# Softmax over rows of 1024: twelve rows per partition and four buffers, in place of eight rows and six

## The chip, the cores and the metric

The kernel runs on one core of a Trainium2 chip. The metric is the device time of one execution in microseconds (us). The kernel before takes 317.45 us, the median of three runs that lie between 317.37 and 318.42 us.

## What is computed

The input `x` has 32 x 512 rows of 1024 float32 numbers, 64 MiB in all, and the temperature is 0.5. Each row is divided by the temperature and goes through a softmax that subtracts the row's maximum first. The output has the shape and type of the input.

```python
scaled = x / temperature
shifted = scaled - np.max(scaled, axis=-1, keepdims=True)
exp_x = np.exp(shifted)
return exp_x / np.sum(exp_x, axis=-1, keepdims=True)
```

So 67.1 MB are read from HBM, 67.1 MB are written to it, and each element is touched by three computations: the maximum, the exponential with its sum, and the multiplication by the sum's reciprocal.

## The kernel before

**Tiles.** The 16384 rows are cut into 16 tiles of 1024 rows. A tile lies in SBUF as 128 partitions with 8 rows each, 32 KiB per partition. The 8 rows of a partition are neighbours in HBM too, so that each partition's share of a transfer is one contiguous piece of 32 KiB (`dram`, L49). Six buffers of this size (`BUFS`, L11) are used in turn, and everything is done in place: a tile is loaded, computed and stored from the same buffer.

**Passes.** A tile is computed in one pass of eight rows, or, for the first two and the last two tiles, in two passes of four (`PASSES`, L13). A pass consists of four steps:

- `maximum` (L62): DVE reduces the rows of the pass to one maximum per row (L68) and scales it to a bias (L71).
- `exponential` (L73): ACT takes one row per instruction (L77) and gives the row's sum as well.
- `divide` (L86): DVE takes the reciprocals (L89), and multiplies the rows by them. Tiles in `WHOLE` (L15: 2, 4, 6, 8, 10 and 12) are multiplied by one instruction for all rows of the pass (L92, TENSOR_TENSOR). Other tiles take one instruction for each row (L95, TENSOR_SCALAR).
- `store` (L99): after the last pass of a tile, ACT's queue issues the store of the whole tile (L107), and the next load is put in order. The very first pass has a store of its own: POOL's queue stores the first row of each partition of tile 0 (L104), so that the store of tile 0 has seven rows.

**Order.** The order is written out by hand. First SP issues six loads (L59). Then, for each pass in turn, the maximum and exponential of this pass come ahead of the division and store of the pass before. From tile 14 on (`ALONE`, L17), the division and the store of the tile before come first when a new tile begins. [...] A load stands on SP and waits until the store of the tile that had its buffer has landed.

**Queues.** Loads run in SP's DMA queue (q1 in the profile), stores in ACT's (q10), and the one piece in POOL's (q0).

Of the kernel before, what the change touches and what calls it, by code (L numbers as in the profile page):

```python
# [1 line left out]

# [4 lines left out]

ROWS = 8  # L10
BUFS = 6  # L11

PASSES = [[4, 4]] * 2 + [[8]] * 12 + [[4, 4]] * 2  # L13

WHOLE = (2, 4, 6, 8, 10, 12)  # L15

ALONE = 14  # L17


@with_exitstack  # L20
def kernel(
    ctx: ExitStack,
    tc: tile.TileContext,
    x: bass.AP,
    temperature: bass.AP,
    out: bass.AP,
):
    nc = tc.nc
    f32 = mybir.dt.float32
    scale = 1.0 / float(temperature)  # L30
    extreme = mybir.AluOpType.max if scale > 0 else mybir.AluOpType.min

    P = 128
    xf = x.flatten_outer_dims()
    of = out.flatten_outer_dims()
    n, d = xf.shape
    assert len(PASSES) * ROWS * P == n

    data = ctx.enter_context(tc.tile_pool(name="data", bufs=BUFS))
    stats = ctx.enter_context(tc.tile_pool(name="stats", bufs=4))  # L40


    groups = []
    for i, ks in enumerate(PASSES):
        assert sum(ks) == ROWS
        for j, k in enumerate(ks):
            groups.append((i, sum(ks[:j]), k))

    def dram(t, i):  # L49
        block = t[P * ROWS * i : P * ROWS * (i + 1), :]  # L50
        return block.rearrange("(p k) d -> p k d", p=P, k=ROWS)

    tiles, small = [], []

    def load():
        i = len(tiles)
        if i < len(PASSES):
            xt = data.tile([P, ROWS, d], f32, name="xt")
            nc.sync.dma_start(out=xt, in_=dram(xf, i))  # L59
            tiles.append(xt)  # L60

    def maximum(g):  # L62
        i, a, k = groups[g]
        top, bias, sums, recip = (
            stats.tile([P, k], f32, name=name) for name in ("top", "bias", "sums", "recip")
        )
        small.append((bias, sums, recip))
        nc.vector.tensor_reduce(  # L68
            out=top, in_=tiles[i][:, a : a + k, :], axis=mybir.AxisListType.X, op=extreme
        )  # L70
        nc.vector.tensor_scalar_mul(bias, in0=top, scalar1=-scale)  # L71

    def exponential(g):  # L73
        i, a, k = groups[g]
        bias, sums, _ = small[g]
        for b in range(k):
            nc.scalar.activation(  # L77
                tiles[i][:, a + b, :],
                tiles[i][:, a + b, :],
                mybir.ActivationFunctionType.Exp,  # L80
                bias=bias[:, b : b + 1],
                scale=scale,
                accum_out=sums[:, b : b + 1],
            )

    def divide(g):  # L86
        i, a, k = groups[g]
        _, sums, recip = small[g]
        nc.vector.reciprocal(recip, sums)  # L89
        if i in WHOLE:  # L90
            xt = tiles[i][:, a : a + k, :]
            nc.vector.tensor_mul(xt, xt, recip.unsqueeze(2).to_broadcast([P, k, d]))  # L92
            return
        for b in range(k):
            nc.vector.tensor_scalar_mul(  # L95
                tiles[i][:, a + b, :], in0=tiles[i][:, a + b, :], scalar1=recip[:, b : b + 1]
            )

    def store(g):  # L99
        i, a, k = groups[g]  # L100


        if g == 0:
            nc.gpsimd.dma_start(out=dram(of, i)[:, :1, :], in_=tiles[i][:, :1, :])  # L104
        elif a + k == ROWS:
            a = 1 if i == 0 else 0
            nc.scalar.dma_start(out=dram(of, i)[:, a:, :], in_=tiles[i][:, a:, :])  # L107
            load()

    with tc.manual_schedule():
        for _ in range(BUFS):
            load()
        for g in range(len(groups) + 1):

            alone = g < len(groups) and groups[g][0] >= ALONE and groups[g][1] == 0
            if g > 0 and alone:
                divide(g - 1)
                store(g - 1)  # L120
            if g < len(groups):
                maximum(g)
                exponential(g)
            if g > 0 and not alone:
                divide(g - 1)
                store(g - 1)


# [1 line left out]
_INS = ['x', 'temperature']  # L130
_OUTS = [((32, 512, 1024), 'float32')]

_NUMBERS = {'temperature': 0.5}


# [26 lines left out]
```

## Time and profile before

| | before |
|---|---|
| median of 3 runs | 317.45 us |
| the profiled execution | 317.44 us |
| its span, from the first to the last instruction or transfer | 315.7 us |
| DVE busy | 251.0 us, 79% |
| ACT busy | 148.1 us, 47% |
| moved over the span | 134.24 MB, mean 425 GB/s |

The profile is of one execution. Its costliest groups of instructions are below. Each line gives the source line, the engine, the operation, what it writes and reads (partitions x elements), how many there are, the busy time in us, the mean of one in ns, and behind the second bar how long the engine had been idle before them and what ended most of that.

```profile
L77 ACT ACTIVATE xt<-xt,bias 128x1024 f32<-128x1024 f32 x128 | 145.2, 1135 | 136.6 <-DVE bias L71 127.1 <-issue 9.6
L68 DVE TENSOR_REDUCE top<-xt 128x8 f32<-128x8192 f32 x12 | 104.2, 8684 | 31.2 <-DMA xt<-in_x_dram 31.2
L95 DVE TENSOR_SCALAR xt<-xt,recip 128x1024 f32<-128x1024 f32 x80 | 54.3, 748 | 0.5
L92 DVE TENSOR_TENSOR xt<-xt,recip 128x8192 f32<-128x8192 f32 x6 | 52.2, 8692 | 0.2
L68 DVE TENSOR_REDUCE top<-xt 128x4 f32<-128x4096 f32 x8 | 35.3, 4412 | 13.2 <-DMA xt<-in_x_dram 13.2
```

A row multiplied by its own TENSOR_SCALAR starts some 0.67 us after the one before (5.39 us for eight), since they overlap a little. In the single TENSOR_TENSOR a row takes 1.09 us.

### The profile page before, as it was taken

The numbers are of one execution on the slowest core, as the hardware profiler recorded it, in microseconds if no ns is written. First come the engines' busy times: TensorE is split into PE (matmuls) and PEld (weight loads), VectorE is DVE, ScalarE is ACT, GpSimd is POOL, SyncE is SP. The second block draws the span as 40 slices with busy tenths as digits, with TensorE's granted clock in tenths as the row PEclk, the third lists the DMA queues.
The fourth block names the chain that finished last, engine by engine and source line by source line (L and its number), as shares of the span: only waits on it lengthen the run. The fifth ranks groups of instructions, "written<-read, shape, count | busy, mean of one in ns | idle before, by whom it ended". The sixth has DMA issues, their size and how long they took to land. (4 is left out here: it accounts for less than half of the span.)

```text
span 315.7 us, 534 instructions
## 1 busy us (share of the span) xinstructions
DVE 251.0 (79%) x146; ACT 148.1 (47%) x257; POOL 1.3 (0%) x5
## 2 busy tenths in 40 slices
DVE  0399999999679795897949979399793999979710
ACT  0176637680906519074290833808247091564700
POOL 0001000000000000000000000000000000000000
DMA  8999999999999999999999999999999999999996
GB/s 328 415 448 421 369 441 434 465 400 461 404 457 407 457 411 457 428 436 436 428 448 415 448 415 449 411 465 403 461 403 461 403 461 403 461 403 461 407 457 274
DMA packets 4755, 134.24 MB, mean 425 GB/s; under 512 B 528, under 2 KB 528, under 8 KB 656
## 3 DMA queue, kind: packets, MB, share of 16 engines
q1 hardware_dynamic: 2304, 67.11, 49.7%
q10 hardware_dynamic: 2304, 66.59, 48.9%
q0 software_dynamic: 144, 0.52, 0.4%
q14 instruction: 3, 0.02, 0.0%
HBM read 67.11 MB, written 67.11 MB: 425 GB/s over the span
## 5 line engine op out<-in xcount | busy, mean ns | idle before, releaser
L77 ACT ACTIVATE xt<-xt,bias 128x1024 f32<-128x1024 f32 x128 | 145.2, 1135 | 136.6 <-DVE bias L71 127.1
L68 DVE TENSOR_REDUCE top<-xt 128x8 f32<-128x8192 f32 (+1 forms) x20 | 139.5, 6976 | 44.4 <-DMA xt<-in_x_dram 44.4
L95 DVE TENSOR_SCALAR xt<-xt,recip 128x1024 f32<-128x1024 f32 x80 | 54.3, 748 | 0.5
L92 DVE TENSOR_TENSOR xt<-xt,recip 128x8192 f32<-128x8192 f32 x6 | 52.2, 8692 | 0.2
L77 ACT ACTIVATION_READ_ACCUMULATOR xt<-xt,bias 128x1 f32 x128 | 23.9, 187 | 0.0
L77 ACT ACT_TABLE_LOAD x1 | 1.3, 1283 | 13.3 <-DMA xt<-in_x_dram 13.3
L89 DVE RECIPROCAL recip<-sums 128x8 f32<-128x8 f32 (+1 forms) x20 | 3.8, 188 | 4.1 <-ACT xt L77 4.1
L71 DVE TENSOR_SCALAR bias<-top 128x8 f32<-128x8 f32 (+1 forms) x20 | 3.4, 171 | 0.7
L104 POOL DMA_DIRECT2D out_dram<-xt x1 | 1.1, 1142 | 23.4 <-DVE xt L95 23.4
L143 POOL MEMSET const-bfloat16-1.0<- 128x1 bf16 x1 | 0.1, 96 | 0.0
L143 POOL MEMSET const-float32-0.0<- 128x1 f32 x1 | 0.1, 93 | 0.2 <-issue 0.2
L143 POOL MEMSET const-float32-1.0<- 128x1 f32 x1 | 0.1, 93 | 0.0
L143 POOL MEMSET const-uint8-127<- 128x1 uint8 x1 | 0.1, 93 | 0.0
## 6 DMA issues: line engine op xcount, KB each, us to landing
xt<-in_x_dram SPq DMA_DIRECT2D x16, 4096.0 KB, 51.2
out_dram<-xt ACTq DMA_DIRECT2D x15, 4096.0 KB, 28.0
out_dram<-xt ACTq DMA_DIRECT2D x1, 3584.0 KB, 23.2
out_dram<-xt POOLq DMA_DIRECT2D x1, 512.0 KB, 19.6
```

What stands on the lines that cost most here:

```text
L68: nc.vector.tensor_reduce(out=top, in_=tiles[i][:, a : a + k, :], axis=mybir.AxisListType.X, op=extreme)
L71: nc.vector.tensor_scalar_mul(bias, in0=top, scalar1=-scale)
L77: nc.scalar.activation(tiles[i][:, a + b, :], tiles[i][:, a + b, :], mybir.ActivationFunctionType.Exp, bias=bias[:, b : b + 1], scale=scal ...
L89: nc.vector.reciprocal(recip, sums)
L92: nc.vector.tensor_mul(xt, xt, recip.unsqueeze(2).to_broadcast([P, k, d]))
L95: nc.vector.tensor_scalar_mul(tiles[i][:, a + b, :], in0=tiles[i][:, a + b, :], scalar1=recip[:, b : b + 1])
L104: nc.gpsimd.dma_start(out=dram(of, i)[:, :1, :], in_=tiles[i][:, :1, :])
L143: nc = _bacc.Bacc("TRN2", target_bir_lowering=False, num_devices=1)
```

## The change

The tiles become larger and their number smaller: ten tiles of twelve rows per partition (pieces of 48 KiB), and a last one of eight rows. There are four buffers instead of six; four times twelve rows take as much of SBUF as six times eight. The first tile is computed in three passes of four rows, the next nine in two passes of six, the last in two passes of four. `WHOLE` names tiles 2, 3, 4, 6 and 8, whose multiplications are now one instruction per pass of six rows. `ALONE` is 9, so that the division and store of the tile before come first for the last two tiles.

Two things are new. Ahead of the store of tile 0, ACT copies one element per partition of tile 2 into a small tile (`seen`), and so waits for the load of tile 2. The stores of tiles 4 and 6 (`HALVES`) are issued as two DMAs each, one of partitions 0 to 63 and one of partitions 64 to 127.

```diff
-ROWS = 8
-BUFS = 6
+PASSES = [[4, 4, 4]] + [[6, 6]] * 9 + [[4, 4]]
+BUFS = 4
-PASSES = [[4, 4]] * 2 + [[8]] * 12 + [[4, 4]] * 2
+WHOLE = (2, 3, 4, 6, 8)
-WHOLE = (2, 4, 6, 8, 10, 12)
+ALONE = 9
-ALONE = 14
+HALVES = (4, 6)
...
+    rows = [sum(ks) for ks in PASSES]
...
     def dram(t, i):
-        block = t[P * ROWS * i : P * ROWS * (i + 1), :]
-        return block.rearrange("(p k) d -> p k d", p=P, k=ROWS)
+        block = t[P * sum(rows[:i]) : P * sum(rows[: i + 1]), :]
+        return block.rearrange("(p k) d -> p k d", p=P, k=rows[i])
...
-        elif a + k == ROWS:
+        elif a + k == rows[i]:
             a = 1 if i == 0 else 0
-            nc.scalar.dma_start(out=dram(of, i)[:, a:, :], in_=tiles[i][:, a:, :])
+            if i == 0:
+                nc.scalar.copy(stats.tile([P, 1], f32, name="seen"), tiles[2][:, 0, 0:1])
+            for p, q in ((0, 64), (64, P)) if i in HALVES else ((0, P),):
+                nc.scalar.dma_start(out=dram(of, i)[p:q, a:, :], in_=tiles[i][p:q, a:, :])
             load()
```

More of the change, by code (lines that the diff above doesn't have):

```diff
@@ L36 @@
     n, d = xf.shape
-    assert len(PASSES) * ROWS * P == n
+    rows = [sum(ks) for ks in PASSES]
+    assert sum(rows) * P == n
     data = ctx.enter_context(tc.tile_pool(name="data", bufs=BUFS))
@@ L44 @@
     for i, ks in enumerate(PASSES):
-        assert sum(ks) == ROWS
         for j, k in enumerate(ks):
@@ L57, in load @@
         if i < len(PASSES):
-            xt = data.tile([P, ROWS, d], f32, name="xt")
+            xt = data.tile([P, rows[i], d], f32, name="xt")
             nc.sync.dma_start(out=xt, in_=dram(xf, i))
```

## The prediction

> **What bounds the kernel now.** I read the head of the page first (span, engines, slices), then the DMA queues, then the same trace cut into stretches, then the waits.
>
> ```profile
> span 315.7 us, 534 instructions
> DVE 251.0 (79%) x146; ACT 148.1 (47%) x257; POOL 1.3 (0%) x5
> DMA  8999999999999999999999999999999999999996
> ...
> q1 hardware_dynamic: 2304, 67.11, 49.7%
> q10 hardware_dynamic: 2304, 66.59, 48.9%
> q0 software_dynamic: 144, 0.52, 0.4%
> ```
>
> No compute engine is full, but the DMA row is at 9 from the second slice to the last but one. The three queues (loads, stores, and the one piece that POOL stores) together took 99.0% of what 16 engines have in the span. The chain of waits covers only 18% of the span, since it ends at ACT and DVE work of the last tiles; here it is not the view that names the bound. The stretches show the rate:
>
> ```profile
> 0.00:2.00 2.00, 0.00 (x0) 0.00 (x0) 0.20 (x4) 1.00 0.67 180
> 2.00:37.00 35.00, 23.43 (x17) 15.09 (x25) 1.14 (x1) 1.00 1.00 417
> 37.00:280.00 243.00, 209.79 (x111) 122.59 (x215) 0.00 (x0) 1.00 1.00 432
> 280.00:312.00 32.00, 17.74 (x19) 10.40 (x19) 0.00 (x0) 1.00 0.99 428
> ```
>
> The columns are the stretch, its length, busy time of DVE, ACT and POOL, the clock, the DMA share and GB/s. Loads alone (second row), both directions (third) and stores alone (fourth) all run at a DMA share of 0.99 to 1.00 and close to one rate. A byte costs the same in either direction, and 134.2 MB at 432 GB/s is 310.7 us. What remains of the span is the 1.8 us before the first packet, 0.7 us by which the first packets are long, the piece of POOL, some 1.0 us by which the last DMA engine ends after the mean one (packet records: 314.5 against 313.5), and 1.2 us after the last packet.
>
> ```profile
> DVE top L68 <- DMA xt<-in_x_dram: 44.4, 10, 13.2
> ...
> SPq L59 <- DMA out_dram<-xt: 214.3, 10, 42.9
> ```
>
> ```profile
> 298.20 2.74 DVE L95 TENSOR_SCALAR xt<-xt,recip 128x1024 f32<-128x1024 f32 x4
> 300.97 0.34 ACTq L107 DMA_DIRECT2D out_dram<-xt  x1
> ```
>
> The first two lines are from the waits (total, times, longest), the last two from the timeline (start, length). DVE waits for loads (44.4 us) and the loads' queue waits for stores to free a buffer (214.3 us): everybody waits for the DMA engines. The last store is issued at 300.97, while the store before it still runs to 304.7 (packet records), so even at the end the engines are not kept waiting.
>
> [...] where both queues have work, the middle stretch, they take nearly equal shares. [...]
>
> **The change, part by part.**
>
> *Pieces of 48 KiB.* Packets: the loads' 2304 are 16 x 144, that is 128 pieces and 16 small ones per load. The packet records give 1213 ns for 32 KiB and 1062 ns for the 28 KiB pieces of the first store; the 4 KiB between them cost 151 ns, so 32 KiB need 1208 and about 5 ns are fixed per packet. One DMA engine moves 256 pieces now and 171 after: 85 x 5 ns = 0.4 us gained. A 48 KiB piece should take 1213 + 4 x 151 = 1817 ns. This is extrapolated; if pieces were cut in two, the 0.4 us is gone, nothing more.
>
> *DVE and ACT.* Rows and passes change, not the work per row. Multiplications in one instruction go from 48 rows to 60: 12 x (8.69/8 - 5.39/8) = 5.0 us more on DVE, which then has about 256 us in 316. In the steady part a tile of 12 rows has 12 x 2 pieces per partition, 8 partitions per engine: 16 x 1.817 = 29.1 us. DVE needs 2 x 6.55 (maxima, between 4.41 for 4 rows and 8.68 for 8) + 0.7 + 13.0 = 26.8 us for a tile multiplied whole and 21.9 for another, ACT 12 x 1.134 = 13.6. Both stay under 29.1, so the DMA engines remain the bound and the cost is 0.
>
> *Four buffers instead of six.* Both hold 48 rows. A steady buffer is loading for 29.1 us, storing for 29.1, computing for about 27; four times 29.1 leaves some 30 us over. A load that comes late doesn't idle the engines while the stores' queue has work.
>
> *The start.* This is the only place where both queues can run dry, and I follow it by shifting the first tiles' times. Load 0 ends 4.8 us later (8 x 0.604), so DVE starts at 18.05 instead of 13.21. With the durations of the timeline: maxima of passes 0 and 1 and the division of pass 0 to 30.3, maximum of pass 2 to 34.7, division of pass 1 to 37.7, first maximum of tile 1 to 44.2, division of pass 2 to 47.3. ACT does the six exponentials of that pass of tile 1 from 44.4 to 51.3. Only then come, in its queue, the new copy and the store of tile 0. The copy waits for load 2, which lands at 1.8 + 0.7 + 3 x 14.54 + 1.2 (POOL's piece) = 47.3; it is no wait at all and costs one small ACT instruction, about 0.2 us by the 187 ns row of 128x1. Were it to bind, the exponentials of tiles 1 and 2 would queue behind it, and DVE behind those. Store 0 goes out at 51.8 instead of 32.9. Until then only loads run, which costs nothing at equal rates. The four loads, POOL's piece and store 0 (11 rows, 8 x 1.666 = 13.3) together keep the engines busy to 1.8 + 0.7 + 58.2 + 1.2 + 13.3 = 75.2, in whichever order. Load 4 can't start before store 0 has landed, so store 1 must be there by 75.2. Its chain: maximum to 53.7, exponentials to 60.8, division of pass 0 to 58.2, maximum of tile 2 to 64.7, exponentials of tile 2 (ahead of the store in ACT's queue) to 71.7, store issued by 72.1. From issue to first packet the trace has 2.2 us (last store) to 3.8 (first store, behind packets in flight): 74.3 to 75.9. So it is 0.9 us early to 0.7 us late; I take 0, and 0.7 for the range.
>
> *Stores after that.* Store 1 ends at about 103, and store 2 is issued at 96; each later margin by the same sums is 9 us or more.
>
> *The end.* Load 10 follows store 6 and ends about 271. Then 3 us of store 7, stores 8 and 9 (14.5 each) and store 10 (9.7) are left, 42 us alone. The compute between the last landing and the last issue took 20 us before (281 to 301). Cost 0; the longer packets make the ends of the DMA engines more ragged, 0.2 us taken, 0 to 0.6 possible.
>
> *Two stores cut by partitions (tiles 4 and 6).* One more issue each, 0.34 us on ACT, hidden. [...] Worst: they move in step and each store packet takes twice as long: 8 packets x 2 tiles x 1.817 = 29 us. The records of before have often 13 engines in one phase and 3 in the other, which speaks for the worst[...]. I take 0 for the likeliest, because a figure for half the partitions alone says little of stores that have only half of each engine's time, and give the loss a case of its own.
>
> Sum on the profiled execution: 315.7 - 0.4 + 0 + 0.2 = 315.5. The run took 1.7 us more than its span (317.44 against 315.7) and equals the median 317.45, so 317.2.
>
> **Rivals.** *Half-partition stores collide* (slower): between 7 and 29 us as above; the middle[...] is 14.5 us, giving 331.7. It decides against "no change" once a split store's packet takes over 1817 + 1600/16 = 1.92 us. Against it: each engine has load packets in between.
> *The start runs dry, or long pieces run below 432 GB/s*: if store 1 is 2.5 us late at 75 us the time is 319.7; pieces 1% slower cost 3.1 us, 320.3. Against it: the sums above, and that 28 and 32 KiB pieces go at one rate.
> [...]
>
> **How the numbers follow.** Forecast 0.62 (its own range 316.2 to 318.5), collision 0.20, start or rate 0.14 (of it 0.03 within half a per cent)[...]. Half a per cent, about what a measurement can tell from no change, is 1.6 us: faster below 315.9, slower above 319.0. So faster 0.04, same 0.65, slower 0.31. [...]
>
> **What would show it.** DMA share 0.99 or more in every stretch from 3 to 310 us, above all around 75, and 432 GB/s in the middle: the forecast. A fall of GB/s between about 160 and 250 us, while tiles 4 and 6 are stored, with long packets there: the collision. A gap in the DMA share near 75: the start. Wrong altogether would be a time under 315, for which the engines would have to move bytes faster than any stretch of before does.

## The result and the profile after

The changed kernel takes 337.23 us (median of six runs), the kernel before 317.36 us beside it. That is 19.9 us slower, where 317.2 was forecast. Without the longest execution the loss is 19.4 us, a ratio of 1.061 with a 95% interval of 1.059 to 1.064. Executions of the changed kernel scatter, from 331.3 to 342.7 us over all that were made; the profile that came with the result is of the longest one (342.69 us), so a second one of the same kernel, 331.3 us long and made apart from the others, is read beside it.

First the head of the page of the first profile, then its DMA queues and the chain of waits by engine.

```profile
span 340.9 us, 517 instructions
...
DVE 257.1 (75%) x147; ACT 148.4 (44%) x258; POOL 1.3 (0%) x5
...
DMA  9999999999999999999999999999999999988780
GB/s 358 398 444 458 406 455 371 424 448 398 450 444 421 427 456 421 416 461 433 346 352 375 341 404 415 444 427 300 358 358 369 381 419 425 434 373 386 342 381 35
...
q10 hardware_dynamic: 1616, 66.59, 48.0%
q1 hardware_dynamic: 1584, 67.11, 47.4%
...
DMA 56%; DVE 27%; ACT 11%; issue 0%; DVEq 0%; SPq 0%
```

DVE's work is 257 us, close to the 256 of the prediction, and ACT's is 148 as before. The DMA row still shows 9 nearly to the end. But the row of GB/s has two dents, slices 20 to 23 and 28 to 32, about where the prediction looked for the sign of a collision (160 to 250 us; slices are 8.5 us long): the engines count as busy there and move 300 to 380 GB/s in place of some 430. From 160 to 200 us the share is 0.99 at 363 GB/s, from 100 to 160 it is 1.00 at 433: the share alone does not show the loss, and the two rows must be read together. The chain of waits leads through DMAs for 56% of the span, but that is no sign of the collision: in the changed kernel without the cut, the first experiment below, it is 51%.

The second profile in stretches (length, busy time of DVE, ACT and POOL, clock, DMA share, GB/s):

```profile
60.00:100.00 40.00, 39.79 (x18) 21.91 (x39) 0.00 (x0) 1.00 1.01 435
100.00:160.00 60.00, 56.04 (x20) 27.70 (x49) 0.00 (x0) 1.00 1.00 434
160.00:200.00 40.00, 28.22 (x19) 20.59 (x36) 0.00 (x0) 1.00 0.98 361
200.00:220.00 20.00, 15.45 (x5) 6.90 (x12) 0.00 (x0) 1.00 1.00 430
220.00:260.00 40.00, 33.62 (x24) 20.70 (x36) 0.00 (x0) 1.00 0.99 372
```

A piece is what a DMA moves for one partition, 48 KiB here, and has one packet in the profiler's records. By these records the two DMAs of tile 4 run from 161 to 201 us, and those of tile 6 are issued at 218 and have landed by 266. Of the stretches shown the rate is low in these two alone; from 60 to 100 us, where the start could have run dry, it is 435. A piece of 48 KiB takes 1.815 us elsewhere; in these two stretches the longest pieces of stores take 3.7 and 4.1 us, and those of the loads beside them lengthen too, to as much as 4.0. In the first profile seven pieces of tile 6 take 4.1 to 7.5 us, more than twice 1.815; why they do is open.

### The profile page after: what moved, and what is told of

It is laid out like the page before. It is cut to its first block, busy times and chain, and to the rows that moved or that the text cites. A ratio compares the mean times of both kernels' runs of the same rounds, so it can differ in the third digit from the quotient of the medians.

```text
span 340.9 us, 517 instructions
## 1 busy us (share of the span) xinstructions
DVE 257.1 (75%) x147; ACT 148.4 (44%) x258; POOL 1.3 (0%) x5
## 4 chain that ended last, share of the span: by engine, by line
DMA 56%; DVE 27%; ACT 11%; issue 0%; DVEq 0%; SPq 0%
DMA xt<-in_x_dram 30%; DMA out_dram<-xt 25%; DVE top L69 17%; ACT xt L78 11%; DVE xt L96 7%; DVE xt L93 2%; DVE bias L72 1%; DVE recip L90 0%; DVEq L163 0%; SPq L60 0%
## 5 line engine op out<-in xcount | busy, mean ns | idle before, releaser
L69 DVE TENSOR_REDUCE top<-xt 128x6 f32<-128x6144 f32 (+1 forms) x23 | 139.9, 6084 | 56.8 <-DMA xt<-in_x_dram 56.8
L93 DVE TENSOR_TENSOR xt<-xt,recip 128x6144 f32<-128x6144 f32 x10 | 65.6, 6558 | 0.6 <-DVE recip L90 0.3
L96 DVE TENSOR_SCALAR xt<-xt,recip 128x1024 f32<-128x1024 f32 x68 | 46.2, 749 | 0.5
L90 DVE RECIPROCAL recip<-sums 128x6 f32<-128x6 f32 (+1 forms) x23 | 4.2, 182 | 5.0 <-ACT xt L78 5.0
L72 DVE TENSOR_SCALAR bias<-top 128x6 f32<-128x6 f32 (+1 forms) x23 | 3.9, 171 | 0.8
## 6 DMA issues: line engine op xcount, KB each, us to landing
out_dram<-xt ACTq DMA_DIRECT2D x1, 4096.0 KB, 19.4
```

Source lines behind the costliest of these rows:

```text
L69: nc.vector.tensor_reduce(out=top, in_=tiles[i][:, a : a + k, :], axis=mybir.AxisListType.X, op=extreme)
L96: nc.vector.tensor_scalar_mul(tiles[i][:, a + b, :], in0=tiles[i][:, a + b, :], scalar1=recip[:, b : b + 1])
```

## The experiments

Two readings stood against each other. **C**: stores of 64 partitions that all lie on one side of partition 64 collide: their packets slow one another down. **S**: the start, the longer pieces or the four buffers cost the time. A third, **N**, is that two DMAs in place of one cost something, whatever they span.

### The changed kernel without the cut

```diff
-HALVES = (4, 6)
+HALVES = ()
```

> The changed kernel with HALVES empty: all stores span 128 partitions. Theory C [...]: the whole loss goes, 316.5 to 318. Rival S (the start, the longer pieces or four buffers cost the time): 325 or more remains. Both in part: between.

Measured: 318.07 us, 1.0024 times the kernel before (1.0012 to 1.0035). Of the 19.9 us, 19.2 go with the cut; S is left with 0.7. The profile of this kernel in the stretches in which tiles 4 and 6 were slow:

```profile
160.00:200.00 40.00, 30.71 (x23) 20.70 (x36) 0.00 (x0) 1.00 1.00 434
200.00:220.00 20.00, 19.86 (x10) 8.42 (x15) 0.00 (x0) 1.00 1.00 433
220.00:260.00 40.00, 34.85 (x20) 19.18 (x34) 0.00 (x0) 1.00 1.00 431
```

Both dents are gone, and the DMA share, 1.00, is hardly higher than with them.

### One cut store

```diff
-HALVES = (4, 6)
+HALVES = (4,)
```

> The changed kernel with the store of tile 4 alone cut by partitions. C, if each cut store costs the same: half of the 19.9 us, 326 to 329. If the second cut store meets DMA engines that the first has put out of step, the first costs less than half (under 325) or more (over 330). S: 337 as with both.

Measured: 326.47 us, 8.4 more than without a cut; the second cut adds 10.8. Its profile has one dent, where tile 4 is stored:

```profile
160.00:200.00 40.00, 28.15 (x19) 20.53 (x36) 0.00 (x0) 1.00 0.99 359
200.00:220.00 20.00, 15.55 (x5) 6.90 (x12) 0.00 (x0) 1.00 1.00 435
220.00:260.00 40.00, 34.43 (x24) 20.70 (x36) 0.00 (x0) 1.00 0.99 426
```

The dent accounts for the loss. The profiled executions of the two kernels are 7.4 us apart (spans of 324.3 and 316.9). Over 40 us the rate is 75 GB/s below the 434 without a cut, 40 x 75/434 = 6.9 us. The rest comes at the end: the last DMA engine ends 2.6 us after the mean one, in the kernel without a cut 1.9 (packet records). The records also show whose packets grew. After 100 us the time beyond 1.815 us per piece comes to 6.6 us for each DMA engine, 4.1 of it in pieces of stores and 2.5 in pieces of loads, although every load spans 128 partitions. Without the cut it is 0.2 us.

### The same two stores, cut by rows

```diff
-for p, q in ((0, 64), (64, P)) if i in HALVES else ((0, P),):
-    nc.scalar.dma_start(out=dram(of, i)[p:q, a:, :], in_=tiles[i][p:q, a:, :])
+for p, q in ((0, 6), (6, 12)) if i in HALVES else ((a, rows[i]),):
+    nc.scalar.dma_start(out=dram(of, i)[:, p:q, :], in_=tiles[i][:, p:q, :])
```

> Stores of tiles 4 and 6 as two DMAs each, but cut by rows (rows 0 to 5 and 6 to 11 of every partition), so that each DMA spans 128 partitions, with pieces of 24 KiB. C: 316.5 to 318, since only the span of partitions matters. Rival N (two DMAs in place of one[...] cost the time): about 337.

Measured: 317.64 us, 1.0011 times before (1.0004 to 1.0018). As many DMAs, in the same places, but each over 128 partitions: nothing is lost. N falls.

### The price by itself: the last store of the kernel before

Here no load runs beside the store that is cut. First at partition 64:

```diff
+HALVES = (15,)
...
-nc.scalar.dma_start(out=dram(of, i)[:, a:, :], in_=tiles[i][:, a:, :])
+for p, q in ((0, 64), (64, P)) if i in HALVES else ((0, P),):
+    nc.scalar.dma_start(out=dram(of, i)[p:q, a:, :], in_=tiles[i][p:q, a:, :])
```

> The kernel before, with only its last store (tile 15, 4 MiB) cut by partitions, where no load runs beside it: the price of the cut alone. [...] the 8 packets of 1.213 us of each engine take twice as long: 9.7 us more, 327. If only a second DMA's fixed cost counts: 318 to 320. [...]

Measured: 326.01 us, 8.65 more than before. The store's stretch:

```profile
304.00:308.00 4.00, 0.00 (x0) 0.00 (x0) 0.00 (x0) 1.00 1.26 279
308.00:312.00 4.00, 0.00 (x0) 0.00 (x0) 0.00 (x0) 1.00 0.64 131
312.00:316.00 4.00, 0.00 (x0) 0.00 (x0) 0.00 (x0) 1.00 1.16 270
316.00:320.00 4.00, 0.00 (x0) 0.00 (x0) 0.00 (x0) 1.00 0.99 205
```

A packet counts where it starts, so single rows swing; the mean of the four is 221 GB/s, about half of the 428 at which the kernel before has stores alone. The median packet of the store takes 2.55 us in the records, where an uncut 32 KiB takes 1.213. The doubling would have cost 9.7 us; about 1 us is not lost. Many of the first and the last packets of each half are shorter (1.2 to 2.3 us); why was not shown.

Then by rows, and in three parts:

```diff
-nc.scalar.dma_start(out=dram(of, i)[:, a:, :], in_=tiles[i][:, a:, :])
+cuts = ((0, 4), (4, 8)) if i == 15 else ((a, ROWS),)
+for p, q in cuts:
+    nc.scalar.dma_start(out=dram(of, i)[:, p:q, :], in_=tiles[i][:, p:q, :])
```

> The kernel before, its last store as two DMAs cut by rows (0 to 3, 4 to 7), each over 128 partitions. C: 317.2 to 318. If the second DMA is what costs in the cut at partition 64: 326.

Measured: 317.67 us, 1.0005 times before (0.9996 to 1.0014): no difference.

```diff
-nc.scalar.dma_start(out=dram(of, i)[:, a:, :], in_=tiles[i][:, a:, :])
+cuts = ((0, 32), (32, 96), (96, P)) if i == 15 else ((0, P),)
+for p, q in cuts:
+    nc.scalar.dma_start(out=dram(of, i)[p:q, a:, :], in_=tiles[i][p:q, a:, :])
```

> The kernel before, its last store cut into partitions 0 to 31, 32 to 95 and 96 to 127. The middle DMA has 64 partitions like each half of the cut at 64, but half of them on either side of partition 64. [...] (C), its packets take 1.21 us and only the two outer DMAs run at half rate: about half of the 8.65 us, 321 to 322.5. If any DMA of fewer than 128 partitions is slow, all packets take 2.4 us or more: 326 or more.

Measured: 320.89 us, 3.6 more than before (1.0085 to 1.0124 times), a little less than the 321 to 322.5 expected. Its stretches:

```profile
304.00:308.00 4.00, 0.00 (x0) 0.00 (x0) 0.00 (x0) 1.00 0.94 238
308.00:312.00 4.00, 0.00 (x0) 0.00 (x0) 0.00 (x0) 1.00 0.99 418
312.00:316.00 4.00, 0.00 (x0) 0.00 (x0) 0.00 (x0) 1.00 1.17 287
```

This is the run that decides what about 64 partitions is slow. The middle DMA also has 64 partitions, but 32 on each side of partition 64, and while it runs the rate is back at 418 GB/s; nearly all of its packets take 1.21 to 1.25 us. The first and the last part, each on one side, are slow, with median packets of 2.0 and 2.4 us. With 64 partitions in each case, 418 GB/s against 221 for the two halves: it isn't the number of partitions that costs here, but that all of them lie on one side of partition 64. The run answers a further question too. A DMA of partitions 0 to 63 writes 2 MiB that lie together in HBM, so the slowness could have come from there; the middle DMA also writes 2 MiB that lie together, and it is fast.

### Beside loads, and for loads

```diff
+HALVES = (6, 9)
```

> The kernel before with the stores of tiles 6 and 9 cut by partitions, both beside loads. C: if a cut store costs the same share of its packets beside loads as tile 4 alone did in the changed kernel (8.4 of 8 x 1.817 = 14.5 us, 0.58), 2 x 0.58 x 9.7 = 11.3 us more, 328.7; 324 to 332 also fits. If smaller tiles and six buffers absorb the collision: under 320.

(With the cut of the stores as above, in the kernel before.) Measured: 326.87 us, the median of four executions between 324.3 and 330.4; without the longest, 1.027 times before (1.020 to 1.034). That is 4.8 us for each cut store, 0.49 of its 9.7, and 0.36 to 0.67 over the four executions, so that no difference from the 0.58 (8.4 of 14.5 us) of the changed kernel's first cut store is shown. Six buffers and smaller tiles don't absorb the collision (9.6 us are lost in all), and the scatter that the changed kernel has appears here too.

```diff
-nc.sync.dma_start(out=xt, in_=dram(xf, i))
+for p, q in ((0, 64), (64, P)) if i == 2 else ((0, P),):
+    nc.sync.dma_start(out=xt[p:q], in_=dram(xf, i)[p:q])
```

> The kernel before with the load of tile 2 cut by partitions at 64; it runs while almost no store does. [...] about 8 us more, 325 to 327. If only reads of SBUF collide: 317.4.

Measured: 326.24 us, 8.9 more than before (1.0255 to 1.0293 times): a load cut at partition 64, which writes to SBUF, is slowed as the store is, which reads from it. The stretch of this load, first in the kernel with the cut, then in the kernel before:

```profile
22.00:32.00 10.00, 9.70 (x13) 6.98 (x13) 1.15 (x1) 1.00 0.93 195
32.00:42.00 10.00, 8.02 (x9) 7.15 (x14) 0.00 (x0) 1.00 1.06 283
```

```profile
22.00:32.00 10.00, 9.68 (x13) 6.98 (x13) 1.14 (x1) 1.00 0.95 408
32.00:42.00 10.00, 9.93 (x10) 7.25 (x14) 0.00 (x0) 1.00 1.07 430
```

### The second profile

> The changed kernel as it is, for a second profile, near the median of its runs. C: packets of up to twice 1.82 us only while tiles 4 and 6 are stored, GB/s down to about 350 there and 430 elsewhere; 336 to 338. S: GB/s down elsewhere too, above all near 75 us.

Measured: 331.3 us in this one execution, below the 336 to 338 expected. The places of the loss are as C has them (shown with the result); its size differs from execution to execution. In the profile of 342.69 us the DMA engines have drifted further apart. Load 9 is done at 264 us on the first DMA engine and at 279 on the last (the trace has 16 landings for each DMA), and the first maximum of tile 9 starts at 279.05, after the last of them. In the shorter profile the two are 5 us apart. At the end the last engine stops 7.4 us after the mean one, in the shorter profile 2.5. What sets this from one execution to the next was not tried.

No kernel that was run beats the kernel before. The variant of the changed kernel that comes nearest, with its cuts by rows, is 0.1% slower.

## Why the prediction was wrong

**The bound.** Right: the DMA transfers remain the bound (a DMA share of 0.98 to 1.01 in the stretches from 60 to 260 us, in both kernels and in the changed one with one cut store and with none), and no kernel that was run gained anything. One reading was off: the chain of waits of the kernel before covers 12% of its span (DVE 6, ACT 6), not 18%. The equal shares of loads and stores hold: from 100 to 200 us of the kernel before they take 50.0 and 50.6% of the engines' time.

**The step that failed** is the one on the two stores cut by partitions: "I take 0 for the likeliest, because a figure for half the partitions alone says little of stores that have only half of each engine's time". No run of before gave such a figure; the last store cut by itself later did, 221 GB/s for 428. Measured, beside loads one cut store of the changed kernel cost 8.4 us (0.58 of its worst case of 14.5) and the second 10.8. Beside loads, with about half of each engine's time, a cut store loses less than alone, 0.49 of a doubling in the kernel before against 0.89 (8.65 of 9.7), but the collision isn't hidden.

The prediction had the collision and its place, and gave the case 0.20. Of its bounds, 7 to 29 us, only the 29 is worked out, from a doubling of the stores' packets that no run of before showed (alone, the median packet of a cut store then took 2.55 us for 1.213); the measured 19.9 us lies between them. The records of before have 11 to 13 of the 16 engines in one phase for seven tenths of the time from 80 to 260 us, which by the prediction's own reasoning spoke against the zero. Priced at its middle, 14.5 us, the term would have given 331.7, still 5.5 too low.

The argument against the collision, that each engine has load packets in between, was never worked out, and the worst case counts packets of stores alone; but of the 6.6 us that one cut store added to the packets, 2.5 were in those of loads. Why they lengthen is open; the packet records don't name a packet's engine.

**Which partitions.** The runs show which partitions are slow together: 221 GB/s for the last store cut into 0 to 63 and 64 to 127, median packets of 2.0 and 2.4 us for 0 to 31 and 96 to 127, and 418 GB/s for 32 to 95, where the kernel before has 428 for stores alone. What the DMA engines wait for in a slow transfer was not shown.

**The rest of the change.** Without the cut, 318.07 was measured against 317.2 forecast for such a case. *Pieces*: 48 KiB took 1.815 us (1.817 worked out), and the packets' time over 16 engines fell from 312.5 to 312.2 us, 0.3 where 0.4 was expected. That this fits is partly luck. The records of all lengths give 9 ns fixed per piece, not 5 (see the last section), and an engine moves 176 pieces in place of 256, not 171; that would be 0.7 us (an estimate from these figures), and longer load packets, most of them among the first, took back the rest, about 0.4 us. *The start*: store 0 was issued at 48.6 us and store 1 at 69.3 (51.8 and 72.1 worked out), and the engines lost less than 0.1 us from 60 to 90 us. The order is not the one worked out:

```profile
48.62 0.38 ACTq L113 DMA_DIRECT2D out_dram<-xt  x1
...
51.49 0.17 ACT L111 COPY seen<-xt 128x1 f32<-128x1 f32 x1
```

The store was issued before the copy ran, and while exponentials ahead of it in ACT's queue still ran. But load 2 landed at 48.59 us (47.3 worked out), 1.1 us after the division that the store needs, and in all five profiles of the changed kernel and its variants the issue follows this landing by 0.02 to 0.03 us. So the copy's wait did hold the store back, by about 1 us, and this cost nothing.

*The end*: load 10 landed at 281 us where 271 was worked out. The last store was issued at 300.2, before the store ahead of it had landed on any engine (303.6), so this cost nothing either. *The ragged end* was mis-sized: the last engine ended 1.9 us after the mean one, where 1.0 plus 0.2 was taken. That is about the size of the 0.7 us over the kernel before; the kernel with its cuts by rows ended with 1.1 and is 0.3 us over. *Four buffers, DVE and ACT*: no cost, as forecast; the rate is 431 to 434 GB/s from 160 to 260 us.

**The other rivals.** The start didn't run dry, and without the cut longer pieces run no slower and reach no higher rate (431 to 436 GB/s in the stretches from 60 to 260 us, 421 to 436 in the kernel before). The 0.04 for a faster kernel stood for longer pieces at a higher rate. The range given, 316.2 to 326 us, left out most of the collision.

## What to carry to other kernels

In a kernel bound by DMA transfers, ask which partitions each transfer spans. Here that was part of its price: stores of all 128 moved at 428 GB/s and one of 32 to 95 at 418 (the only such span that was run), but a store cut at partition 64 at 221. Cut by rows instead, stores cost 0.3 and 0.4 us (317.64 and 317.67 us in all), within 0.2% of the kernel before; that is the cut to try first. And where a prediction names a mechanism with bounds of 0 and a large loss, and the profile speaks for the loss, the zero needs an argument as worked out as the loss.

## What the runs showed of the hardware

- A store of 4 MiB cut at partition 64 moved at 221 GB/s with no load beside it (428 uncut), and a load cut so lost as much (8.65 and 8.9 us); a DMA of partitions 32 to 95 ran at 418 GB/s.
- While cut stores run beside loads, the DMA engines count as busy: a share of 0.98 to 1.00 at 359 to 372 GB/s, where 431 to 434 were moved at 1.00 without the cut.
- The cost of a piece is nearly proportional to its length: 0.159 us for 4 KiB, 0.611 for 16, 0.912 for 24, 1.062 for 28, 1.213 for 32, 1.665 for 44 and 1.815 for 48. All seven lie within 1 ns of 9 ns plus 150.5 ns for each 4 KiB, so about 9 ns per piece are all that longer pieces saved.
- A collision outlived its store. In the changed kernel with one cut store, the next store, itself not cut, landed 14.3 us later on its last DMA engine than on its first; without a cut this was 2.2 us. The kernels with two cut stores beside loads scatter by 6 us (324.3 to 330.4) and 11 us (331.3 to 342.7) between executions, those without a cut at partition 64 by less than 1.5.
